# Output projection of an encoder trunk: eight blocks of full products, against two groups of seven products on chained weights

## The chip, the cores and the metric

One core of a Trainium2 chip runs the whole program. The metric is the device time of one execution in microseconds (us); the time before is the median of three runs, 1547.62 us (1545.86 to 1549.45).

## What is computed

A trunk of two layers works on 512 tokens of 1024 channels in float32. Each layer computes four branches (a convolution module and three kinds of attention), projects each to 1024 channels, mixes them by gates, applies one output projection and adds the residual; then a feed-forward block with a short convolution follows.

```python
h = _rmsnorm(x, g_mix[l])
proj = h @ w_in[l]
...
branch = jnp.einsum('bsnc,ncd->bsnd', ys, w_branch[l])
gates = jax.nn.sigmoid(gate_pre.reshape(bsz, seq, N_BRANCH, D_MODEL) + gate_b[l])
mixed = jnp.sum(gates * branch, axis=2)
x = x + mixed @ w_out[l]
x = x + _conv_ffn(_rmsnorm(x, g_ffn[l]), w_up[l], ffn_conv_w[l], ffn_conv_b[l], w_down[l])
```

The change concerns `mixed @ w_out[l]`: a product of 512 x 1024 with 1024 x 1024.

## The kernel before

**Layout.** Activations lie channel by channel: a tile has 128 channels on the partitions and the 512 tokens along it, so eight tiles hold one activation. A float32 product is made of three matmuls of rounded parts: high by high, high by low and low by high (`prod`, L274 to L279). So each weight and each activation is split into a high part, made by ScalarE (ACT), and a low part, made by VectorE (DVE).

**Weights.** They stream in units of 128 x 1024, two units ahead of use (`weights`, L226; `unit`, L262). SyncE's queue (SP) loads `w_raw` (two buffers), ACT makes `w_hi` (L256) and DVE makes `w_lo` (L258), with three buffers each. A buffer of w_hi or w_lo is free when the product that read it three units ago is done, and the instruction that fills it waits for that at its place in its engine's order.

**Gates.** For each of four branches and each of eight blocks d, PE makes the gate's pre-activation (24 matmuls into a `mm` bank), DVE scales it (`t`, L845), ACT takes the tanh (L847), PE makes the branch projection, DVE multiplies (L874), and GpSimd (POOL) adds the result to `mx` (L875; for the last branch's blocks 6 and 7, DVE does). With the last branch, block d of the mixture is complete, and ACT and DVE make its parts mh (L879) and ml (L880).

**Output projection** (in `layer`, L1466 to L1480). Eight blocks of output channels, each 8 x 3 matmuls of 512 columns, 192 a layer. The first two blocks are cut so that the last two mixed tiles are needed last. Behind each block `update` adds the residual (`xr`, loaded over SP's queue), writes the new residual (L929), and `norm_tile` prepares the next norm: ACT's xh (L339) and squares (L348), DVE's xl (L340) and sum of squares `sqacc` (L349). After the eighth, `broadcast_norm` sums the squares over the channels on PE (L367), and DVE runs Newton steps for the reciprocal root (L311 to L316) into `RB`.

**Up projection** (`ffn`). It begins with eight full blocks, whose results stay in `mm` banks until DVE has RB and evacuates them into `U` (L1081). Then come groups of seven products: for a 2 x 2 partition of weights and activations, seven products of combined parts replace eight. The seven weight combinations of a group are chained: A11 is loaded, split and used, then another quarter of the weights is added onto the same buffer by an accumulating load on POOL's queue (`grow`, L1123), which gives S3, then S2, then S4; likewise A22 gives S1 (`seven_unit`, L1126). One product is 24 matmuls of 256 columns and accumulates into one of three banks (A, B, C) of its group. ACT copies a bank to `sv` (L1007) before a later product accumulates further into it. The activations' combinations (`seven_forms`, L936) are made by DVE and ACT beside.

**Down sums.** The down projection needs sums of weight quarters, made in DRAM by 24 copying and accumulating transfers a layer on POOL's queue (`weight_sums`, L1148). They are dealt out during the attention and gates: each tick adds the pace (4.0, later 2.7) to a budget, and each transfer takes 11 from it.

**What sets the order.** A scheduler orders the instructions of each engine by priorities; weights stand high. Within an engine the order is then fixed, and an instruction that waits holds all behind it on that engine. PSUM has four `mm` and four `aux` banks.

## Time and profile before

| | |
|---|---|
| median of three runs | 1547.62 us (1545.86 to 1549.45) |
| the profiled execution | 1548.55 us, span 1546.8 us, mean PE clock 0.998 |
| busy share of the span | PE 99%, DVE 81%, ACT 58%, POOL 12% |
| output projection, layer 0 | 391.5 to 439.8 us |
| output projection, layer 1 | 1162.1 to 1205.6 us |
| first eight up blocks begin | 439.8 and 1205.6 us |

A row of a timeline gives the start in us, the duration, the engine, the line, the operation, what it writes and reads, and in brackets how long the engine was idle before and for whom it waited. PE is the matmul, PEld its weight load. The ends of matmuls are modelled, so a matmul's cost is read from the spacing of starts. A row of grouped instructions ends with total and mean time.

### The profile page before, as it was taken

How to read it: one execution, taken by the hardware profiler on the slowest of the kernel's cores; microseconds unless marked ns; L12 is line 12 of the kernel's file. 1: busy time of each engine (PE TensorE's matmuls, PEld its weight loads, DVE VectorE, ACT ScalarE, POOL GpSimd, SP SyncE). 2: the span in 40 equal slices, each digit the busy share in tenths (PEclk: the TensorE clock that was granted, in tenths of full speed). 3: DMA queues.
4: the chain of work that ended last, by engine and by line, in shares of the span. 5: the costliest groups of instructions: out<-in, count | busy, mean ns of one | idle time of the engine just before them, and what ended most of it. 6: DMA issues, size and time to landing. Idle time of an engine off the chain costs nothing.

```text
span 1546.8 us, 22163 instructions
## 1 busy us (share of the span) xinstructions
PE 1535.4 (99%) x7986; PEld 1313.9 (85%) x7986; DVE 1256.5 (81%) x2126; ACT 904.7 (58%) x1516; POOL 190.8 (12%) x276
## 2 busy tenths in 40 slices
PE   9999999999999999999999999999999999999998
PEld 8888888887789999888888888888888899988887
DVE  6689988764579998997586899887646899999974
ACT  6677777343456665564457777673334556655643
POOL 0113002222101110000001120022221011100000
PEclk9999999999999999999999999999999999999999
DMA  7767654647655886356558776546576589853675
GB/s 232 228 212 158 130 157 131 157 166 134 200 191 123 185 183 164 96 196 202 185 184 252 196 150 138 152 134 157 160 164 219 170 180 228 182 160 95 191 229 159
DMA packets 114142, 268.05 MB, mean 173 GB/s; under 512 B 26992, under 2 KB 28912, under 8 KB 114032
## 3 DMA queue, kind: packets, MB, share of 16 engines
q1 hardware_dynamic: 87664, 190.08, 38.4%
q0 software_dynamic: 26080, 76.03, 26.2%
q8 instruction: 63, 1.03, 0.3%
q10 hardware_dynamic: 288, 0.52, 0.1%
q14 instruction: 47, 0.39, 0.1%
HBM read 248.76 MB, written 58.72 MB: 199 GB/s over the span
## 4 chain that ended last, share of the span: by engine, by line
PE 88%; DMA 4%; DVE 4%; ACT 3%; issue 1%; POOL 0%; SPq 0%; ACTq 0%; DVEq 0%; POOLq 0%
PE mm L278 16%; PE mm L277 16%; PE mm L279 16%; PE aux L995 11%; PE aux L1240 3%; PE aux L1241 3%; PE aux L1242 3%; PE mm L506 2%; PE mm L507 2%; PE mm L508 2%; DMA chain<-W 2%; PE mm L1240 2%; PE mm L1241 2%; PE mm L1242 2%; PE aux L799 2%; DMA w_raw<-W 2%
## 5 line engine op out<-in xcount | busy, mean ns | idle before, releaser
L256 ACT ACTIVATE w_hi<-w_raw 128x1024 fp32r<-128x1024 f32 (+1 forms) x257 | 268.4, 1044 | 299.0 <-PE mm L278 142.0
L258 DVE TENSOR_TENSOR w_lo<-w_raw,w_hi 128x1024 fp32r<-128x1024 f32 (+1 forms) x257 | 310.1, 1208 | 87.2 <-ACT w_hi L256 85.3
L277 PE MATMUL mm<-xh,w_hi 128*128 128x512 f32 x896 | 350.5, 391 | 0.7 <-ACT w_hi L256 0.7
L279 PE MATMUL mm<-xh,w_lo 128*128 128x512 f32 x896 | 349.4, 390 | 0.5 <-DVE w_lo L258 0.5
L278 PE MATMUL mm<-xl,w_hi 128*128 128x512 f32 x896 | 349.4, 390 | 0.0
L279 PEld LDWEIGHTS mm<-xh,w_lo 128*128 128x128 f32 x896 | 168.2, 188 | 36.7 <-DVE w_lo L258 1.0
L277 PEld LDWEIGHTS mm<-xh,w_hi 128*128 128x128 f32 x896 | 168.3, 188 | 34.9 <-ACT w_hi L256 1.1
L278 PEld LDWEIGHTS mm<-xl,w_hi 128*128 128x128 f32 x896 | 168.4, 188 | 33.3
L995 PE MATMUL aux<-form,w_hi 128*128 128x256 f32 x768 | 140.2, 284 | 1.1 <-ACT sv L1007 1.1
L995 PEld LDWEIGHTS aux<-form,w_hi 128*128 128x128 f32 x768 | 120.0, 192 | 2.3 <-ACT sv L1007 1.9
L995 PE MATMUL aux<-form,w_lo 128*128 128x256 f32 x384 | 108.7, 283 | 0.0
L444 DVE SCALAR_TENSOR_TENSOR cv<-cv,prm 128x512 f32<-128x512 f32 x120 | 93.6, 780 | 0.7
L1036 ACT ACTIVATE cy<-U,prm 128x512 f32<-128x512 f32 x88 | 68.4, 808 | 31.8 <-DVE U L1081 21.0
L875 POOL TENSOR_TENSOR mx<-mx,t 128x512 f32<-128x512 f32 x44 | 65.2, 1489 | 167.7 <-DVE t L874 152.5
L845 DVE TENSOR_TENSOR t<-mm,RB 128x512 f32<-128x512 f32 x64 | 43.8, 685 | 45.0 <-PE mm L279 44.8
L506 PE MATMUL mm<-w_hi,xh 128*128 128x512 f32 x192 | 76.4, 398 | 0.4 <-DVE V L634 0.4
L507 PE MATMUL mm<-w_lo,xh 128*128 128x512 f32 x192 | 75.0, 391 | 0.0
L508 PE MATMUL mm<-w_hi,xl 128*128 128x512 f32 x192 | 74.8, 390 | 0.0
L1141 ACT ACTIVATE w_hi<-chain 128x1024 fp32r<-128x1024 f32 x48 | 50.7, 1057 | 39.9 <-DMA chain<-W 12.7
L995 PEld LDWEIGHTS aux<-form,w_lo 128*128 128x128 f32 x384 | 73.7, 192 | 0.0
L1150 POOL DMA_DIRECT2D sums<-W x36 | 31.8, 882 | 313.9 <-PE mm L279 165.6
L763 ACT ACTIVATE e<-e,rl 128x256 f32<-128x256 f32 (+2 forms) x96 | 57.4, 598 | 21.8 <-DVE rl L762 21.4
(343 smaller groups left out, 3469.0 us busy)
## 6 DMA issues: line engine op xcount, KB each, us to landing
w_raw<-W SPq DMA_DIRECT2D x199, 512.0 KB, 3.9
sums<-W POOLq DMA_DIRECT2D x24, 1024.0 KB, 11.0
chain<-W POOLq DMA_DIRECT2D x36, 512.0 KB, 5.6
w_raw<-W SPq DMA_DIRECT2D x66, 256.0 KB, 3.8
w_raw<-sums SPq DMA_DIRECT2D x44, 256.0 KB, 3.8
w_raw<-sums SPq DMA_DIRECT2D x22, 512.0 KB, 4.0
sums<-W POOLq DMA_DIRECT2D x12, 768.0 KB, 9.2
sums<-sums POOLq DMA_DIRECT2D x8, 1024.0 KB, 8.2
```

The source lines that it names most:

```text
L256: w = nc.scalar.activation(hi[:, s], raw[:, s], AF.Copy)
L258: nc.vector.tensor_tensor(lo[:, s], raw[:, s], hi[:, s].bitcast(F32), ALU.subtract)
L277: mm(ps, lhsT=wh, rhs=xh, start=start, stop=False)
L278: mm(ps, lhsT=wh, rhs=xl, start=False, stop=False)
L279: self.last_mm = mm(ps, lhsT=wl, rhs=xh, start=False, stop=stop)
L444: self.after_mm(v.scalar_tensor_tensor(acc, u[:, t:t + S], w(t), acc, ALU.mult, ALU.add))
L506: mm(pss[b], lhsT=self.Xh[k][:, t], rhs=hi[:, s], start=k == 0, stop=False)
L507: mm(pss[b], lhsT=self.Xh[k][:, t], rhs=lo[:, s], start=False, stop=False)
L508: self.last_mm = mm(pss[b], lhsT=self.Xl[k][:, t], rhs=hi[:, s], start=False, stop=k == KT - 1)
L995: self.last_mm = nc.tensor.matmul(o, lhsT=w[:, s], rhs=x, start=start and not (e or j or i), stop=j == 3 and i == 2, skip_group_check=True)
L1240: mm(ps, lhsT=x[0], rhs=w[0][:, cols], start=start, stop=False, skip_group_check=again)
L1241: mm(ps, lhsT=x[0], rhs=w[1][:, cols], start=False, stop=False, skip_group_check=again)
```

## The change

The output projection becomes two groups, `oa` and `ob` (output channels 0 to 511 and 512 to 1023), of seven products each, of the same kind as the up projection's: 14 products of 24 matmuls of 256 columns, 336 a layer. The order of the products is written out in `OUT_STEPS`; the first three are cut so that the last pair of mixed tiles is needed last. The weights are chained: A11's buffer has two of its own ("chain"), A22 and A12 use w_raw. The combinations of the mixed tiles are made in the gates of the last branch, by `mixed_forms` after each odd d. The residual is loaded by POOL's queue into four tiles before the last branch's end, and written by it. The norm tiles come in the order 0, 1, 4, 5, 2, 3, 6, 7, all behind the products S1 and S4. A down sums transfer takes 9 from the budget instead of 11.

```diff
+OUT_STEPS = [('oa', 'A11'), ('oa', 'A12'), ('ob', 'A11'), ('ob', 'A12'), ('oa', 'S3'), ('oa', 'A22'), ('ob', 'S3'),
+             ('ob', 'A22'), ('oa', 'S2'), ('oa', 'S1'), ('ob', 'S2'), ('ob', 'S1'), ('oa', 'S4'), ('ob', 'S4')]
...
-        self.Xh, self.Xl = [], []
+        self.Xh, self.Xl = [None] * KT, [None] * KT
...
+            if d % 2 == 1:
+                self.mixed_forms(d // 2)
+
+    def mixed_forms(self, j):
...
+        x, y = self.mixed[2 * j:2 * j + 2]
+        t = self.op.tile([P, 1024], F32, name="sums", tag="msum", bufs=1)
+        t1, t2, t3, t4 = (t[:, n * 256:(n + 1) * 256] for n in range(4))
+        b11, b12, b21, b22 = x[:, :256], x[:, 256:], y[:, :256], y[:, 256:]
+        v.tensor_tensor(t3, b12, b22, ALU.subtract)
+        v.tensor_tensor(t1, b11, b12, ALU.subtract)
+        v.tensor_tensor(t2, t3, b11, ALU.subtract)
+        v.tensor_tensor(t4, b21, t2, ALU.add)
+        hi, lo = (self.op.tile([P, 1024], F32R, name="mform", tag=f"mf{2 * j + n}", bufs=1) for n in range(2))
+        nc.scalar.activation(hi, t, AF.Copy, scale=0.5)
+        v.scalar_tensor_tensor(lo, t, 0.5, hi.bitcast(F32), ALU.mult, ALU.subtract)
...
+    def out_bank(self, g, n):
+
+        b = g, {'S3': 'B', 'A22': 'B', 'A12': 'C'}.get(n, 'A')
...
+    def out_part(self, g, n, w, js):
+
+        ps = self.out_bank(g, n)
+        for e in range(2):
+            o = ps[:, e * 256:(e + 1) * 256]
+            for j in js:
+                s = slice((2 * j + e) * P, (2 * j + e + 1) * P)
+                xh, xl = self.out_x(n, j)
+                for i, (a, x) in enumerate(((w[0], xh), (w[0], xl), (w[1], xh))):
...
+    def out_done(self, g, n):
...
+        if n in ('A11', 'S3', 'S2'):
+            tag, bufs = ("t1", 2) if n == 'S3' else ("th", 3)
+            t = self.svs[g, n] = self.gp.tile([P, S], F32, name="sv", tag=tag, bufs=bufs)
+            with self.first():
+                nc.scalar.activation(t, ps, AF.Copy)
+        if n == 'S2':
+            r, h = 1, 0
+            v.tensor_tensor(t, self.out_bank(g, 'S3'), t, ALU.subtract)
+        elif n == 'A12':
+            r, h, t = 0, 0, self.svs[g, 'A11']
+            v.tensor_tensor(t, t, ps, ALU.add)
+        elif n == 'S1':
+            r, h, t = 1, 1, self.svs[g, 'S3']
+            with self.first():
+                v.tensor_tensor(t, t, ps, ALU.subtract)
+        elif n == 'S4':
+            r, h, t = 0, 1, ps
...
+        v.tensor_tensor(o, two(t), o, ALU.add)
+        if h:
+            for e in range(2):
+                xn = x[:, e * S:(e + 1) * S]
+                nc.gpsimd.dma_start(self.xnew[d + e], xn)
+                self.norm_tile(d + e, xn, self.op)
+
+    def out_projection(self):
...
+                self.nc.gpsimd.dma_start(x[:, e * S:(e + 1) * S], self.xres[d + e])
...
             if n == 'A11':
-                raw = self.fp.tile([P, 1024], F32, name="chain", tag="w_more", bufs=2)
+                pool, tag = (self.op, "chain") if g in ('oa', 'ob') else (self.fp, "w_more")
+                raw = pool.tile([P, 1024], F32, name="chain", tag=tag, bufs=2)
...
-                yield 11
+                yield 9
...
-                for d in range(0, KT, 2):
...
-                            if k1 == KT:
-                                self.update(d + e, pss[e], self.op)
+                self.out_projection()
```

Three places of the order follow, where numbers behind a name tell tiles apart. The first is ACT in the output projection. Before, each weight split stands alone, among the parts of the norm (xh, sq):

```order
L256 ACTIVATE w_hi<-w_raw 128x1024
L339 ACTIVATE xh_4264<-xn,prm 128x512
L348 ACTIVATE sq<-xn 128x512
L256 ACTIVATE w_hi<-w_raw 128x1024
L339 ACTIVATE xh_4306<-xn,prm 128x512
L348 ACTIVATE sq<-xn 128x512
```

After, in the same place, from the split of S2 of group oa (w_hi_4421) to that of S4 of group ob (w_hi_4605); sv_4419 is the copy of ob's S3, sv_4478 that of oa's S2, and w_hi_4450, 4482, 4527 and 4559 are S1 of oa, S2 and S1 of ob, and S4 of oa:

```order
L1249 ACTIVATE w_hi_4421<-chain_4076 128x1024
L1249 ACTIVATE w_hi_4450<-w_raw_4324 128x1024
L944 ACTIVATE sv_4419<-aux_4394 128x512
L1249 ACTIVATE w_hi_4482<-chain_4217 128x1024
L1249 ACTIVATE w_hi_4527<-w_raw_4387 128x1024
L944 ACTIVATE sv_4478<-aux_4198 128x512
L1249 ACTIVATE w_hi_4559<-chain_4076 128x1024
L1249 ACTIVATE w_hi_4605<-chain_4217 128x1024
```

A copy now stands behind one or two weight splits, each of which waits for a buffer that PE still reads. PE's order there is A22 of oa, 9 matmuls of S3 of ob, 5 of S2 of oa, A22 of ob, 19 of S2 of oa, 13 of S2 of ob, S1 of oa, 11 of S2 of ob, 4 of S4 of oa, S1 of ob, 20 of S4 of oa, S4 of ob; ahead of these, 10 of S3 of oa, 2 of S3 of ob, 14 of oa, 13 of ob.

The second place is DVE around the first evacuation of the up projection (U) and the last Newton step (rs_q, RB). Before:

```order
L315 TENSOR_TENSOR rs_q<-rs_q,ms 128x512
L258 TENSOR_TENSOR w_lo<-w_raw,w_hi 128x1024
L316 SCALAR_TENSOR_TENSOR RB<-rs_q,RB 128x512
L961 TENSOR_TENSOR forms<-xf,forms 128x256
L1081 TENSOR_TENSOR U_4490<-mm,RB 128x512
L1081 TENSOR_TENSOR U_4493<-mm,RB 128x512
L964 TENSOR_TENSOR form<-forms,form 128x1024
```

After:

```order
L321 TENSOR_TENSOR rs_q<-rs_q,ms 128x512
L1250 TENSOR_TENSOR w_lo<-chain,w_hi 128x1024
L322 SCALAR_TENSOR_TENSOR RB<-rs_q,RB 128x512
L1067 TENSOR_TENSOR forms<-forms,xf 128x256
L1188 TENSOR_TENSOR U_4702<-mm,RB 128x512
L1068 TENSOR_TENSOR forms<-xf,forms 128x256
L1188 TENSOR_TENSOR U_4705<-mm,RB 128x512
```

The w_lo in front of the last Newton step is now that of the first chained product (chain, L1250), which follows the fourth up block on PE and takes a buffer that this block reads; before, it stood five rows behind the first U (L1142), and the one in front belonged to a full block. On PE, 16 matmuls of that chained product now stand between the fourth and the fifth block.

The third place is POOL in the last branch's gates, with the last transfers of the down sums. Before:

```order
L875 TENSOR_TENSOR mx<-mx,t_3895 128x512
L1150 DMA sums_681<-W 512x512
L875 TENSOR_TENSOR mx<-mx,t_3945 128x512
L875 TENSOR_TENSOR mx<-mx,t_3994 128x512
L1150 DMA sums_682<-W 384x512
L875 TENSOR_TENSOR mx<-mx,t_4050 128x512
L875 TENSOR_TENSOR mx<-mx,t_4099 128x512
```

After:

```order
L880 TENSOR_TENSOR mx<-mx,t_3447 128x512
L1258 DMA sums_681<-W 512x512
L880 TENSOR_TENSOR mx<-mx,t_3529 128x512
L1258 DMA sums_682<-W 384x512
L880 TENSOR_TENSOR mx<-mx,t_3580 128x512
L880 TENSOR_TENSOR mx<-mx,t_3658 128x512
L880 TENSOR_TENSOR mx<-mx,t_3703 128x512
```

The last transfer is followed by two adds before and by nine after; the residual's eight loads (L976) stand a few rows further ahead, between adds.

More of the change, by code (lines that the diff above doesn't have):

```diff
@@ L110, in weight_units @@
                 units.append(('branch', (n, d // 4), 1024))
-    for d in range(8):
-        units.append(('out', d, 1024))
+    units.extend(('quarter', (key, r, c), 1024) for key in ('oa', 'ob') for r in range(2) for c in range(2))
     for g in range(NP2):
@@ L143, in pack_weights @@
                 g, r, c = a
-                src = w_up[l].reshape(4, 2, P, 2, NP2, 2, P)[:, c, :, 1 - r, g].transpose(1, 0, 2, 3)
+                if g in ('oa', 'ob'):
+                    src = w_out[l].reshape(4, 2, P, 2, 2, 2, P)[:, c, :, 'ab'.index(g[1]), 1 - r]
+                else:
+                    src = w_up[l].reshape(4, 2, P, 2, NP2, 2, P)[:, c, :, 1 - r, g]
+                src = src.transpose(1, 0, 2, 3)
             elif kind == 'quad':
@@ L147, in pack_weights @@
             else:
-                w, c = {'in_d': (w_in, a), 'up': (w_up, a), 'out': (w_out, 0 if kind != 'out' else a * P)}[kind]
+                w, c = {'in_d': (w_in, a), 'up': (w_up, a)}[kind]
                 src = w[l][:, c:c + P].reshape(8, P, P).transpose(1, 0, 2)
@@ new lines, in out_x @@
+    def out_x(self, n, j):
+        form = {'S1': 0, 'S2': 1, 'S3': 2, 'A22': 3}.get(n)
+        if form is not None:
+            return [t[:, form * 256:(form + 1) * 256] for t in self.mforms[j]]
+        r, h = {'A11': (0, 0), 'A12': (1, 0), 'S4': (1, 1)}[n]
+        return [t[:, h * 256:(h + 1) * 256] for t in self.MH[2 * j + r]]
+    def out_bank(self, g, n):
+        b = g, {'S3': 'B', 'A22': 'B', 'A12': 'C'}.get(n, 'A')
+        if b not in self.banks:
+            self.banks[b] = self.mm() if b[1] == 'C' else self.aux()
+        return self.banks[b]
@@ new lines, in out_part @@
+    def out_part(self, g, n, w, js):
[6 more added lines that the diff above has]
+                for i, (a, x) in enumerate(((w[0], xh), (w[0], xl), (w[1], xh))):
+                    start = n in ('S3', 'A11', 'A12') and not (e or j or i)
+                    self.last_mm = self.nc.tensor.matmul(o, lhsT=a[:, s], rhs=x, start=start, stop=j == 3 and i == 2,
+                                                         skip_group_check=True)
@@ new lines, in out_done @@
+    def out_done(self, g, n):
+        nc = self.nc
+        v = nc.vector
+        ps = self.out_bank(g, n)
+        if n in ('A11', 'S3', 'S2'):
[15 more added lines that the diff above has]
+            r, h, t = 0, 1, ps
+        else:
+            return
+        d = 4 * 'ab'.index(g[1]) + 2 * (1 - r)
+        x = self.residual[d // 2]
+        two = lambda t: t.rearrange("p (e q) -> p e q", e=2)
+        o = two(x)[:, :, h * 256:(h + 1) * 256]
+        v.tensor_tensor(o, two(t), o, ALU.add)
[4 more added lines that the diff above has]
+                self.norm_tile(d + e, xn, self.op)
@@ new lines, in out_projection @@
+    def out_projection(self):
+        self.banks, self.svs, self.residual = {}, {}, []
+        for d in range(0, KT, 2):
+            x = self.op.tile([P, 1024], F32, name="xr", tag=f"xr{d}", bufs=1)
+            for e in range(2):
+                self.nc.gpsimd.dma_start(x[:, e * S:(e + 1) * S], self.xres[d + e])
+            self.residual.append(x)
+        ws = []
+        for js in ((0, 1, 2), (3,)):
+            for i, (g, n) in enumerate(OUT_STEPS[:3]):
+                if js[0] == 0:
+                    ws.append(self.unit())
+                self.out_part(g, n, ws[i], js)
+                if js[0] == 3:
+                    self.out_done(g, n)
+        for g, n in OUT_STEPS[3:]:
+            self.out_part(g, n, self.unit(), range(4))
+            self.out_done(g, n)
@@ L1167, in weight_sums @@
                 add(part(t, d), part(src, s), accum_op=ALU.add)
-                yield 11
+                yield 9
         for d, b, s in ((s2, s3, b21), (s4, s2, b22)):
@@ L1365, in run @@
                         self.w_list.append((n, lambda src=src: [src]))
+                self.w_list.extend(('seven', (l, g, n)) for g, n in OUT_STEPS)
                 for kind, a, b in UP_STEPS:
@@ L1426, in layer @@
         last = l == L - 1
-        self.Y, self.mixed, self.MH, self.glu_u = [None] * 4, [], [], []
+        self.Y, self.mixed, self.MH, self.mforms, self.glu_u = [None] * 4, [], [], [], []
         with tc.tile_pool(name="gate", bufs=1, reuse_waits="tile") as self.gp:
@@ L1465, in layer @@
                 self.start_norm('g_ffn')
-                for d in range(0, KT, 2):
-                    cuts = (0, KT - 2, KT) if d == 0 else (0, KT)
-                    pss, ws = [self.mm(), self.mm()], []
-                    for k0, k1 in zip(cuts, cuts[1:]):
-                        for e in range(2):
-                            if k0 == 0:
-                                ws.append(self.unit())
-                            hi, lo = ws[e]
-                            for k in range(k0, k1):
-                                s = slice(k * P, (k + 1) * P)
-                                self.prod(pss[e], hi[:, s], lo[:, s], self.MH[k][0], self.MH[k][1], k == 0,
-                                          k == KT - 1)
-                            if k1 == KT:
-                                self.update(d + e, pss[e], self.op)
+                self.out_projection()
                 self.xres = self.xnew
```

10 lines of the change are left out of this document (6 added, 4 removed).

## The prediction

> **What bounds the kernel now.** I read the chain of work that ended last first: it says which engine sets the end.
>
> ```profile
> PE 88%; DMA 4%; DVE 4%; ACT 3%; issue 1%; POOL 0%; SPq 0%; ACTq 0%; DVEq 0%; POOLq 0%
> ```
>
> TensorE (PE) sets the end, so a microsecond counts only if PE has fewer columns to stream or waits less. Second, what PE waits for over the whole span (total, times, longest):
>
> ```profile
> PE mm L277 <- ACT mh L879: 2.5, 1, 2.5
> ...
> PE aux L995 <- ACT sv L1007: 1.1, 2, 0.8
> PE mm L277 <- ACT w_hi L256: 0.7, 1, 0.7
> PE mm L279 <- DVE w_lo L258: 0.5, 1, 0.5
> ```
>
> PE hardly waits anywhere; of what it does wait, the mh, w_hi and w_lo rows (3.7 us) belong to one place, at the output projection. Third, four stretches with each engine's busy time (instructions), the PE clock, the DMA share and GB/s: the output projection of layer 0, the 22 us behind it, the same two of layer 1, and a piece of the first.
>
> ```profile
> 391.50:439.80 48.30, 45.72 (x194) 37.12 (x193) 29.63 (x37) 19.78 (x27) 5.42 (x12) 0.96 0.63 206
> 439.80:462.10 22.30, 22.30 (x100) 18.44 (x100) 20.18 (x33) 14.00 (x19) 0.54 (x1) 1.00 0.52 177
> 1162.10:1205.60 43.50, 43.50 (x193) 36.04 (x192) 26.74 (x34) 18.14 (x26) 4.46 (x12) 1.00 0.67 220
> 1205.60:1228.00 22.40, 22.40 (x100) 18.55 (x99) 20.29 (x34) 14.11 (x19) 0.54 (x1) 1.00 0.58 199
> 392.00:404.00 12.00, 9.42 (x34) 7.05 (x33) 8.06 (x10) 4.40 (x6) 1.54 (x5) 0.86 0.28 98
> ```
>
> Layer 1's projection has no hole: 43.5 us, PE busy throughout. Layer 0's is 4.8 us longer. Behind it DVE is busy 90% of the time (20.2 of 22.3), in it about 60%.
>
> **PE's stream.** The projection is now 192 matmuls of 512 columns a layer and becomes 2 x 7 x 24 = 336 of 256. The spacing of each kind, from the first and last of 18 and of 16 matmuls in a row:
>
> ```profile
> 435.76 0.39 PE L277 MATMUL mm<-mh,w_hi 128*128 128x512 f32 x1
> ...
> 439.61 0.39 PE L279 MATMUL mm<-mh,w_lo 128*128 128x512 f32 x1
> ```
> ```profile
> 539.77 0.28 PE L995 MATMUL mm<-xh,w_lo 128*128 128x256 f32 x1
> ...
> 541.57 0.28 PE L995 MATMUL mm<-xh,w_lo 128*128 128x256 f32 x1
> ```
>
> 3.85/17 = 0.2265 us and 1.80/15 = 0.120 us. So 192 x 0.2265 = 43.5 becomes 336 x 0.120 = 40.3: 3.2 us less a layer, not the eighth (5.4) that the column count says, since the narrow matmul costs more per column. [...]
>
> **New waits inside the stage.** I walk the after order with these durations: what passes from PE to ACT to DVE when a weight buffer comes free, and from PE to ACT when a bank is copied.
>
> ```profile
> 439.39 0.39 PE L278 MATMUL mm<-ml,w_hi 128*128 128x512 f32 x1
> 439.61 0.39 PE L279 MATMUL mm<-mh,w_lo 128*128 128x512 f32 x1
> 439.81 1.06 ACT L256 ACTIVATE w_hi<-w_raw 128x1024 fp32r<-128x1024 f32 x1 [3.24 <-PE mm L278]
> 440.91 1.22 DVE L258 TENSOR_TENSOR w_lo<-w_raw,w_hi 128x1024 fp32r<-128x1024 f32 x1 [0.18 <-ACT w_hi L256]
> 442.05 0.74 DVE L340 SCALAR_TENSOR_TENSOR xl<-xn,prm,xh 128x512 fp32r<-128x512 f32 x1
> ...
> 547.33 0.28 PE L995 MATMUL aux<-form,w_lo 128*128 128x256 f32 x1
> 547.66 0.59 ACT L1007 ACTIVATE sv<-aux 128x512 f32<-128x512 f32 x1
> ```
>
> ACT starts 0.42 after the releasing 512-wide matmul and 0.33 after a 256-wide one, so 0.21 after its slot ends. w_hi's last reader is a product's last matmul but one: ACT splits w_hi from 0.09 after the product's end, done at 1.15 (PE may go at 1.20); DVE's w_lo is done at 2.4 (PE at 2.45). A copy (0.59) behind a w_hi on ACT comes at 0.09 + 0.97 + 0.59 + 0.05 = 1.7. DVE starts its next operation 1.14 after a 1024-wide one. What PE has in between, by the after order:
>
> - S2a's weights wait for A22a's buffer. Cover: 9 matmuls of S3b = 1.08. Wait 0.12 for w_hi; two matmuls later (1.44) 1.0 for w_lo: **1.1**.
> - S4a's weights wait for S1a's. Cover: 11 of S2b and two of S4a = 1.56; but two 512-wide DVE operations of S1a's result stand ahead of the w_lo, which comes at 0.21 + 2 x 0.60 + 1.22 + 0.05 = 2.7: 1.1. Then S1b needs the copy of S2b, which ACT makes behind two w_hi, at 1.32 + 1.7 = 3.0, and PE is there at 2.9: 0.1 to 0.2. **1.3**.
> - S3a to A22a, and S2a to S1a: the copy at 1.7, cover 13 matmuls = 1.56: **0.13** each.
> - The head. The forms of the mixed rows stand on DVE in front of the second group's weights.
>
> ```profile
> 458.92 0.68 DVE L316 SCALAR_TENSOR_TENSOR RB<-rs_q,RB 128x512 f32<-128x512 f32 x1
> 459.52 0.41 DVE L961 TENSOR_TENSOR forms<-xf,forms 128x256 f32<-128x256 f32 x1
> 459.86 1.28 DVE L1081 TENSOR_TENSOR U<-mm,RB 128x512 f32<-128x512 f32 x2
> ```
> ```profile
> 1161.11 1.30 POOL L875 TENSOR_TENSOR mx<-mx,t 128x512 f32<-128x512 f32 x1 [5.31 <-DVE t L874]
> ```
>
> A 512-wide operation takes 0.60, a 256-wide 0.34. In layer 1 the first form that needs mx5 can go when POOL has it, at 1162.41. From there to the end of A12b's w_lo DVE has 7 operations of 256, 6 of 512 and 3 of 1024: 2.4 + 3.6 + 3.4 = 9.4, at 1171.9. PE, started at 1162.1, wants it after 74 matmuls (8.9), at 1171.0. With 0.2 to 0.4 for ACT's parts in between: **1.3**.
>
> Sum 1.1 + 1.3 + 0.3 + 1.3 = **4.0** a layer. From below 1.3 (the head alone, if ACT and DVE run ahead), from above 6: DVE goes from 26.7 to about 40 busy of 44 us (six more w_lo, 6 x 1.14, and some three forms, each 4 x 0.34 + 1.14), so any slip stays. I take the walked value.
>
> **Behind the stage.** In the old kernel the fifth up block takes a bank that U's first evacuation frees, at 459.86 + 0.64 = 460.5, ahead of need (PE waits for nothing in that stretch). In the new order the w_lo of the first chained up product stands ahead of the last Newton step and of U on DVE, and waits until the fourth block has released its buffer. From that block's end: w_hi released at 0.42 less two slots, so at -0.03, done at 1.03; w_lo 1.07 to 2.29; last Newton step, form and U (2.21 + 0.60 + 0.34 + 0.68): 3.8. PE holds 16 matmuls of the chained product for it (1.9), which themselves wait for the same w_hi (1.08) and w_lo (1.0). They end at 4.0: **2.1** lost. Add **0.2** for the last norm tiles, now four at the end instead of one, whose xl the first up block needs. From below 0.2, from above 3.5.
>
> Both layers alike: -3.2 + 4.0 + 2.3 = +3.1, twice = **+6.2**.
>
> **Layer 0's stall.** Three rows show where it comes from, and the clock behind it; then the DMA issues (count, size, median us to landing) in the 45 us ahead of the projection, of layer 0 and of layer 1.
>
> ```profile
> 380.12 1.06 ACT L256 ACTIVATE w_hi<-w_raw 128x1024 fp32r<-128x1024 f32 x1 [6.22 <-DMA w_raw<-W]
> ...
> 392.71 1.06 ACT L256 ACTIVATE w_hi<-w_raw 128x1024 fp32r<-128x1024 f32 x1 [5.24 <-DMA w_raw<-W]
> ...
> 397.75 0.63 PE L277 MATMUL mm<-mh,w_hi 128*128 128x512 f32 x1 [2.49 <-ACT mh L879]
> ...
> 401.51 0.39 PE L279 MATMUL mm<-mh,w_lo 128*128 128x512 f32 x1
> ```
> ```profile
> w_raw<-W SPq DMA_DIRECT2D x6, 512.0 KB, 9.5
> sums<-W POOLq DMA_DIRECT2D x2, 1024.0 KB, 15.0
> ```
> ```profile
> w_raw<-W SPq DMA_DIRECT2D x8, 512.0 KB, 4.1
> sums<-W POOLq DMA_DIRECT2D x1, 1024.0 KB, 11.6
> ```
>
> The weights land late beside the down sums' transfers, ACT waits, and mh comes late. From 397.75 to 401.51 eight matmuls take 3.76 instead of 1.81: after a wait of 2.5 the clock was halved for that long, 1.95 us. The place costs 4.8 (48.3 - 43.5) + 0.7 + 0.5 = **6.0**. With 9 instead of 11 a step the sums end seven POOL adds earlier in the order, and two of these adds stand 6.8 apart:
>
> ```profile
> 1140.71 1.28 POOL L875 TENSOR_TENSOR mx<-mx,t 128x512 f32<-128x512 f32 x1 [1.46 <-DVE t L874]
> 1147.51 1.29 POOL L875 TENSOR_TENSOR mx<-mx,t 128x512 f32<-128x512 f32 x1 [5.51 <-DVE t L874]
> ```
>
> That is about 48 us: the last sums transfer is gone before the late stretch begins. Against it: layer 1 has sums there too and no stall. The residual's loads, 2 MB, now come over POOL's queue in the stretch that the sums leave. I take the 6.0 whole, with the other end, 0, as a rival.
>
> **Costed at nothing.** The chained weights are accumulating loads, of which the up stage has 36; the last column is their median time to landing.
>
> ```profile
> chain<-W POOLq DMA_DIRECT2D x36, 512.0 KB, 5.6
> ```
>
> The eight new ones a layer take 5.6 us each and then 1.06 + 1.22 for the split, against four products (11.5) between two uses of one chain. The residual's loads and writes leave SP's queue for POOL's, whose adds are off PE's path until mx5; 14 weight transfers of 512 KB replace 8, and 2 MB of loads leave the stage: about 1 MB more in 44 us, 24 GB/s on 220. If these covers go, a late chain costs up to 2 us a layer.
>
> **Sum:** 1548.55 (the profiled execution; span 1546.8 and the rest around it) + 6.2 - 6.0 = **1548.8**. The median of the runs is 0.9 below that execution, with 3.6 between the runs; I leave the sum there.
>
> **Rivals.** (1) *Faster: the waits don't show.* In the up stage the same chained products run with the same copies, and PE lost 1.1 us in two waits over two layers. If the fill covers here too, only the head stays: -3.2 + 1.3 + 0.2 = -1.7 a layer, with layer 0's 6.0: 1539.2. Against it: the covers counted above (1.1, 1.6, 1.9) are shorter than 2.45, and the chained w_lo stands ahead of U. Chance 0.25. (2) *Slower: the clock falls at the new stalls.* Place: behind the fourth up block, 1.1 + 1.0 of waiting in 4 us; price 1.95 a layer as at 397.75; it decides if two short waits count like one of 2.5. 1548.8 + 3.9 = 1552.7. [...] Chance 0.17. (3) *No relief:* the late weights of layer 0 aren't the sums' doing or move elsewhere: 1548.55 + 6.2 = 1554.8. For it: layer 1. Against: landing 9.5 against 4.1 with two to three sums transfers in the stretch. Chance 0.18.
>
> **How the numbers follow.** Forecast 0.40, its own range 1545.5 to 1552 (waits 1.5 us a layer either way). The range for 8 in 10, 1540 to 1556, leaves out the lower half of (1) and the tail of (3). 0.2%, about what a measurement can tell, is 3.1 us: below 1544.5 or above 1550.7. Faster: 0.25 + 0.02 = 0.27. Slower: 0.10 of the forecast, 0.14 of (2), 0.17 of (3) = 0.41. Same: 0.32.
>
> **What would show it.** Right: a projection of 44 to 45 us in both layers, PE waits on w_lo at S2a, S4a and A12b of about 1 us each, and a wait on w_hi, then w_lo, behind the fourth up block; layer 0 as long as layer 1. Wrong: projection near 41 (rival 1), clock under 1 behind the stage (2), layer 0's stretch ahead still with w_raw at 9 us (3), or waits on the chain's DMA, which I priced at nothing.

## The result, and the profile after

The changed kernel takes 1565.63 us (median of four runs, 1563.95 to 1571.04) against 1547.67 us (1545.86 to 1549.45): a ratio of 1.0116, 95% interval 1.0104 to 1.0128, so 18 us slower. The forecast was 1548.8 in a range of 1540 to 1556. The profiled execution is the slowest of the four, 1571.04, with a span of 1569.3. A second profile of the same kernel, below called "again", has a span of 1561.0.

What PE waits for in the changed kernel (total, times, longest) answers to the same view of before:

```profile
PE aux L1102 <- DVE w_lo L1250: 6.3, 3, 3.0
PE aux L932 <- DVE w_lo L1250: 3.7, 4, 1.1
PE aux L932 <- ACT sv L944: 3.6, 2, 1.9
PE aux L1102 <- ACT w_hi L1249: 3.5, 2, 2.3
PE mm L932 <- DVE w_lo L1250: 1.6, 2, 0.8
PE mm L932 <- DVE ml L885: 1.4, 2, 0.7
```

L932 is the output projection. L1102 is the chained up products; all but 0.3 us of its rows stands at the first of them, behind the fourth up block. The old waits of layer 0 (mh, w_hi and w_lo of the full blocks, 3.7 us) are gone; 20 us of new ones stand there, half in the projection and half behind it. The stretches, with each engine's busy time, the clock, the DMA share and GB/s; of each layer first the projection, then from its end to the fifth up block; first the profiled execution, then again, then the kernel before with only the pace of the down sums changed:

```profile
389.50:439.50 50.00, 44.99 (x338) 43.43 (x337) 35.40 (x46) 25.35 (x33) 9.41 (x12) 0.93 0.62 137
439.50:470.40 30.90, 26.59 (x116) 21.36 (x115) 27.61 (x45) 18.61 (x26) 7.56 (x17) 0.92 0.72 244
1169.60:1218.80 49.20, 43.98 (x338) 42.38 (x338) 35.36 (x46) 25.20 (x32) 9.39 (x12) 0.97 0.62 139
1218.80:1250.90 32.10, 26.61 (x116) 21.39 (x115) 27.64 (x46) 18.77 (x27) 7.44 (x17) 0.94 0.74 251
```
```profile
389.90:435.40 45.50, 42.18 (x337) 40.79 (x337) 35.13 (x46) 25.14 (x32) 9.43 (x12) 1.00 0.66 150
435.40:467.00 31.60, 26.77 (x117) 21.52 (x116) 27.82 (x46) 19.05 (x28) 7.54 (x17) 0.93 0.73 240
1166.30:1211.80 45.50, 42.18 (x337) 40.80 (x336) 35.11 (x46) 25.16 (x32) 9.36 (x12) 1.00 0.68 150
1211.80:1243.50 31.70, 26.62 (x116) 21.42 (x115) 27.68 (x46) 18.80 (x27) 7.41 (x17) 0.90 0.76 255
```
```profile
389.50:433.00 43.50, 43.50 (x194) 36.02 (x193) 26.70 (x34) 18.16 (x26) 4.41 (x12) 1.00 0.70 223
433.00:455.20 22.20, 22.20 (x100) 18.38 (x99) 20.15 (x33) 13.91 (x19) 0.54 (x1) 1.00 0.51 175
```

Read the third against the second. The projection is 45.5 us instead of 43.5. From its end to the fifth up block PE needs 31.6 instead of 22.2, and the 16 chained matmuls done there account for 1.9 of it: 7.5 us lost. Together 9.5 a layer, 19 in two; the down sums give back 4.8 (first experiment, by its ratio); that leaves 14, where again was measured at 15.1 (1564.63 against 1549.51). Span against span, again is 20.7 us longer than the third profile (1561.0 against 1540.3): 19, and 1.4 more in the fifth up block, whose first matmuls still run at half clock (0.43 us apart instead of 0.23). The first execution has 4.5 and 3.7 us more in its two projections. So three things are to be explained: 2 us in the projection, some 4 more in some executions, and 7.5 behind it.

**Behind the projection.** Two things come late. The first is the norm. All eight norm tiles now stand behind S1 and S4, and the sum of squares that the norm starts from is complete later; ACT's copy of it (sqh), before and after:

```profile
443.43 0.63 ACT L362 ACTIVATE sqh<-sqacc 128x512 fp32r<-128x512 f32 x1 [1.42 <-DVE sqacc L349]
```
```profile
449.23 0.63 ACT L367 ACTIVATE sqh<-sqacc 128x512 fp32r<-128x512 f32 x1 [1.29 <-DVE sqacc L354]
```

That is 3.6 us behind the projection's end before and 9.8 after; both kernels show the same in layer 1. The first U, the end of the norm's chain, started 20.1 us behind the projection and now starts 28.6 to 29.8 behind it. So 6.2 of some 9 us are there when the norm begins, and the rest, 2.5 to 3.6, comes on its way.

The second is the reload. POOL before:

```profile
416.65 0.57 POOL L946 DMA_DIRECT2D xf<-res  x1 [6.95 <-DMA res<-xn]
...
443.28 0.54 POOL L946 DMA_DIRECT2D xf<-res  x1 [4.86 <-DMA res<-xn]
```

And the timeline of the changed kernel in layer 0, POOL, ACT, DVE and PE:

```profile
443.55 2.14 POOL L967 DMA_DIRECT2D res<-xr  x4 [4.42 <-DVE xr L963]
...
451.33 0.54 POOL L1053 DMA_DIRECT2D xf<-res  x1 [4.44 <-DMA res<-xr]
452.05 2.78 POOL L1053 DMA_DIRECT2D xf<-res  x5 [0.19 <-issue]
```
```profile
457.59 2.09 ACT L1060 ACTIVATE xf<-xf,prm 128x512 f32<-128x512 f32 x3 [1.21 <-DMA xf<-res]
459.58 1.05 ACT L262 ACTIVATE w_hi<-w_raw 128x1024 fp32r<-128x1024 f32 x1
...
462.70 1.04 ACT L1249 ACTIVATE w_hi<-chain 128x1024 fp32r<-128x1024 f32 x1
```
```profile
460.66 1.23 DVE L264 TENSOR_TENSOR w_lo<-w_raw,w_hi 128x1024 fp32r<-128x1024 f32 x1 [0.94 <-ACT w_hi L262]
...
466.01 1.22 DVE L1250 TENSOR_TENSOR w_lo<-chain,w_hi 128x1024 fp32r<-128x1024 f32 x1
...
468.09 0.68 DVE L1188 TENSOR_TENSOR U<-mm,RB 128x512 f32<-128x512 f32 x1
```
```profile
463.80 0.38 PE L1102 MATMUL aux<-xh,w_hi 128*128 128x256 f32 x1 [1.16 <-ACT w_hi L1249]
...
467.29 0.58 PE L1102 MATMUL aux<-xh,w_lo 128*128 128x256 f32 x1 [2.98 <-DVE w_lo L1250]
...
468.09 0.41 PE L1102 MATMUL aux<-xh,w_lo 128*128 128x256 f32 x1
468.30 0.41 PE L1102 MATMUL aux<-xh,w_hi 128*128 128x256 f32 x1
```

The up projection's forms read the residual back from DRAM (`seven_forms`, `xf`). Before, it was written block by block, and one reload followed each write, the first at 409 us. Now six of its eight loads are issued at 451 to 455 us, behind the last writes. ACT's scalings of xf then stand, waiting, ahead of two weight splits; DVE waits for the first of these, does the forms and Newton steps queued behind it, and starts the chained w_lo 3.3 us after its w_hi was begun. PE waits 1.2 and 3.0 us, and when it goes on, one 256-wide matmul takes 0.21 us instead of 0.12. Two slices of 5 us show the clock behind it:

```profile
465.00:470.00 5.00, 2.71 (x12) 2.72 (x13) 4.97 (x10) 1.19 (x2) 0.90 (x1) 0.52 0.22 24
470.00:475.00 5.00, 5.00 (x20) 4.20 (x20) 5.00 (x9) 3.19 (x4) 0.00 (x0) 0.80 0.43 81
```

Of the first slice PE works 2.7 us at half speed (1.3 lost); the second loses 1.0.

The spacing of PE's starts in again says what the 7.5 us are: 5.0 in layer 0 and 5.2 in layer 1 are the two waits (for the chained w_hi and w_lo), 0.7 goes in the first up block, whose matmuls meet the last norm tiles, and some 1.7 are the matmuls at half clock or just behind a wait.

**In the projection, in some executions.** ACT and POOL of the changed kernel, then PE, and then ACT of again:

```profile
423.78 1.06 ACT L1249 ACTIVATE w_hi<-chain 128x1024 fp32r<-128x1024 f32 x1 [3.10 <-PE aux L932]
427.10 1.06 ACT L1249 ACTIVATE w_hi<-chain 128x1024 fp32r<-128x1024 f32 x1 [2.26 <-DMA chain<-W]
428.06 0.58 ACT L944 ACTIVATE sv<-aux 128x512 f32<-128x512 f32 x1
```
```profile
419.47 0.89 POOL L1231 DMA_DIRECT2D chain<-W  x1 [4.90 <-DVE w_lo L1250]
```
```profile
426.50 0.39 PE L932 MATMUL aux<-mh,w_lo 128*128 128x256 f32 x1 [1.08 <-DVE w_lo L1250]
426.72 0.28 PE L932 MATMUL aux<-mh,w_hi 128*128 128x256 f32 x1
428.69 0.80 PE L932 MATMUL aux<-mform,w_hi 128*128 128x256 f32 x2 [1.69 <-ACT sv L944]
429.29 0.41 PE L932 MATMUL aux<-mform,w_lo 128*128 128x256 f32 x1
```
```profile
424.21 1.06 ACT L1249 ACTIVATE w_hi<-chain 128x1024 fp32r<-128x1024 f32 x1 [3.10 <-PE aux L932]
425.53 1.06 ACT L1249 ACTIVATE w_hi<-chain 128x1024 fp32r<-128x1024 f32 x1 [0.26 <-PE aux L932]
426.50 0.58 ACT L944 ACTIVATE sv<-aux 128x512 f32<-128x512 f32 x1
```

The load that makes ob's S4 out of its S2 is issued at 419.47, when S2's w_lo is done, and has landed at 427.1, 7.6 us later; ACT's split waits for it, and the copy `sv`, which PE needs for S1 of ob, stands behind that split. Two waits of 1.1 and 1.7 us with one pair of matmuls between them halve the clock once more (granted 0.50 from 428.7 to 433.0). In again the load is in time, ACT waits only for PE's buffer, and the wait on the copy is absent in both layers. The profiles of all versions that keep this load, 14 with two layers each, show it late in 9 of 28 projections: ACT's split then begins 6.7 to 7.8 us behind the issue, else at most 5.7.

### The profile page after: what moved, and what is told of

The parts are those of the page before. It is cut to its first block, busy times and chain, and to the rows that moved or that the text cites. A ratio compares the mean times of both kernels' runs of the same rounds, so it can differ in the third digit from the quotient of the medians.

```text
span 1569.3 us, 22886 instructions
## 1 busy us (share of the span) xinstructions
PE 1542.2 (98%) x8274; PEld 1330.1 (85%) x8274; DVE 1297.0 (83%) x2190; ACT 931.4 (59%) x1548; POOL 225.5 (14%) x324
## 3 DMA queue, kind: packets, MB, share of 16 engines
q0 software_dynamic: 30944, 92.81, 29.8%
## 5 line engine op out<-in xcount | busy, mean ns | idle before, releaser
L262 ACT ACTIVATE w_hi<-w_raw 128x1024 fp32r<-128x1024 f32 (+1 forms) x241 | 251.3, 1043 | 241.9 <-PE mm L284 84.6
L264 DVE TENSOR_TENSOR w_lo<-w_raw,w_hi 128x1024 fp32r<-128x1024 f32 (+1 forms) x241 | 291.3, 1210 | 76.8 <-ACT w_hi L262 75.3
L1102 PE MATMUL aux<-form,w_hi 128*128 128x256 f32 x768 | 140.0, 283 | 0.0
L1102 PEld LDWEIGHTS aux<-form,w_hi 128*128 128x128 f32 x768 | 120.0, 192 | 0.7 <-ACT sv L1114 0.4
L1102 PE MATMUL aux<-form,w_lo 128*128 128x256 f32 x384 | 108.7, 283 | 0.0
L1250 DVE TENSOR_TENSOR w_lo<-chain,w_hi 128x1024 fp32r<-128x1024 f32 x64 | 78.0, 1220 | 28.4 <-ACT w_hi L1249 28.2
L1249 ACT ACTIVATE w_hi<-chain 128x1024 fp32r<-128x1024 f32 x64 | 67.4, 1055 | 56.5 <-DMA chain<-W 21.8
L1231 POOL DMA_DIRECT2D chain<-W x48 | 42.3, 881 | 258.3 <-DVE w_lo L1250 251.0
L1102 PEld LDWEIGHTS aux<-form,w_lo 128*128 128x128 f32 x384 | 73.7, 192 | 0.0
```

What stands on the lines that cost most here:

```text
L262: w = nc.scalar.activation(hi[:, s], raw[:, s], AF.Copy)
L264: nc.vector.tensor_tensor(lo[:, s], raw[:, s], hi[:, s].bitcast(F32), ALU.subtract)
L1102: self.last_mm = nc.tensor.matmul(o, lhsT=w[:, s], rhs=x, start=start and not (e or j or i), stop=j == 3 and i == 2, skip_group_check=True)
L1250: nc.vector.tensor_tensor(lo, raw, hi.bitcast(F32), ALU.subtract)
```

## The experiments

Times of a group of runs are compared with the kernel before on the same chip, 1548.9 to 1549.7 us there. The changed kernel was measured again in one of these groups, with a ratio of 1.0107 (1.0082 to 1.0133).

**The down sums' pace alone.** In the kernel before:

```diff
-                yield 11
+                yield 9
```

> The kernel before with 9 instead of 11 a transfer of the down sums, and nothing else: one part of the change alone. Theory A (the sums' transfers make layer 0's weights late): the stall ahead of and in layer 0's output projection goes, 6 us, about 1541.7. Rival (that lateness is not the sums' doing or only moves): within 1.5 us of 1547.7.

1543.03 us, ratio 0.9969 (0.9955 to 0.9983), which is 4.8 us; the medians differ by 5.8 (1548.86 in its group). PE's waits of layer 0 are gone and its projection is 43.5 us like layer 1's. In the 45 us ahead of it there is no sums transfer left, and the weights land in 3.4 us, where they took 9.5:

```profile
w_raw<-W SPq DMA_DIRECT2D x8, 512.0 KB, 3.4
```

Theory A holds. This is also the fastest version of all, faster than both kernels.

**The reload without its wait on the writes.** The forms read the residual of before the projection:

```diff
-                nc.gpsimd.dma_start(x[:, e * S:(e + 1) * S], self.xres[2 * j + e])
+                nc.gpsimd.dma_start(x[:, e * S:(e + 1) * S], self.xold[2 * j + e])
```

> The changed kernel in the same order of instructions, but the up projection's forms read the residual of before the output projection (so those forms hold other numbers), and their eight loads wait for no write. Theory A (behind the stage the late reload of the residual holds ACT, and with it the weight splits, Newton and U): PE's waits there, 4.1 and 5.3 us, fall to about 2.1 each and the halved clock behind them goes in part, 1555 to 1560. Rival B (the chained w_lo ahead of U on DVE is the whole cause): the waits stay, within 1.5 us of the changed kernel.

1562.51 us, ratio 1.0088 (1.0065 to 1.0110): not told apart from the changed kernel, and PE's waits behind the stage stay (1.7 and 3.0 the longest). But it was a weak test: the loads still stand behind the writes' issue on POOL, and ACT scaled the first xf at 450 us, 14.4 us after the projection's end. It told nothing against the reload.

**S4 without the accumulating load.**

```diff
-        if n[0] == 'A':
+        own = g in ('oa', 'ob') and n == 'S4'
+        if n[0] == 'A' or own:
...
+            nc.sync.dma_start(raw, q(1, 2) if own else q(int(n[1]), int(n[2])))
...
-        if more:
+        if more and not (g in ('oa', 'ob') and n == 'S2'):
```

> The changed kernel, but S4 of both output groups uses a quarter loaded over SP's queue instead of the accumulated chain, and the accumulating load on S2 is left out (the output projection's numbers are others). Theory A (the accumulating load of ob's S4 lands late, ACT's split of it waits, and the copy of S2 that PE needs stands behind that): PE's wait on the copy, 1.7 and 1.9 us, falls under 0.5 and the halved clock after it, some 2.4 us each, goes: 1557 to 1562. Rival (the order on ACT alone makes that wait): the wait stays, within 1.5 us of the changed kernel.

1566.56 us, ratio 1.0116 (1.0101 to 1.0131): no gain. The wait on the copy is gone in this profile and the projection 45.5 us in both layers, but behind it the fifth block starts 33 to 34 us after the projection's end instead of 31.6, of which 1.0 is eight more chained matmuls ahead of it: the four more loads over SP's queue take w_raw's two buffers, and the up blocks' weights come late (PE waits 1.0 and 1.5 us for the w_hi of a full block, and not at all in again). And since again shows 45.5 us with the accumulating load too, the absence can't be put down to this edit. What it shows is the price of the other way to load.

**U ahead of the chained w_lo.** The split of the first chained up product is put behind the first U (`u0`):

```diff
-        nc.scalar.activation(hi, raw, AF.Copy)
-        nc.vector.tensor_tensor(lo, raw, hi.bitcast(F32), ALU.subtract)
+        with self.tc.issue_after(self.u0.ins) if (g, n) == (SEVEN[0], 'A11') else nullcontext():
+            nc.scalar.activation(hi, raw, AF.Copy)
+            nc.vector.tensor_tensor(lo, raw, hi.bitcast(F32), ALU.subtract)
```

> The changed kernel, but the first chained up product's weights are split only behind the first evacuation of U, which takes the w_lo out of the way of the last Newton step; PE then has no chained product to fill the wait. Theory B (this order is the cause of the stall behind the stage): the stall falls to 1 us or so, 1553 to 1558. Theory A (the reload holds ACT and DVE anyway): U comes only 1.1 us earlier and the fill of 1.9 us is lost, within 3 us of the changed kernel.

1567.29 us, ratio 1.0118. PE now waits 7.5 us (3.7 the longest) for U itself; the fifth block starts at 29.1 and 29.4 us, 2.4 and 2.3 earlier than in again, of which 1.7 are 14 chained matmuls that are not done by then. Theory B, that the order of w_lo and U is the cause, is out: U itself starts only 0.8 to 0.9 us earlier.

**The changed kernel again.**

> The changed kernel once more, for a second profile. Theory A (the accumulating load of ob's S4 lands at the edge of its need): the wait on the copy of S2 differs between executions, so it can be absent here, and the output projection is then 45.5 instead of 49 to 50 us; the stall behind the stage stays at 30 to 32 us from the projection's end to the fifth block. Rival: both as in the first profile.

1564.63 us, ratio 1.0107. As shown above: no wait on the copy, projection 45.5 us twice, fifth block at 31.5 and 31.7 us. Theory A on the accumulating load holds so far that its lateness comes and goes; what makes it land in 7.6 us in one execution and in at most 5.6 in another was not found; the transfers issued in the next 8.5 us are the same in both profiles, one weight load and two residual writes.

**Forms from xh.** No reload and no scaling:

```diff
-                for e in range(2):
-                    s = slice(e * S, (e + 1) * S)
-                    nc.scalar.activation(x[:, s], x[:, s], AF.Copy, scale=self.par('g_ffn', 2 * j + e))
...
+                x, y = (t.bitcast(F32) for t in self.Xh[2 * j:2 * j + 2])
```

> The changed kernel, with the up projection's forms made from the high part xh, which lies in SBUF, so the reload of the residual (eight loads) and ACT's eight scalings are left out, and the low part is missing in those forms. Theory A (the late reload holds ACT and DVE): U comes about 2.5 us earlier after the projection's end (29.5 to 27), PE's wait there falls from 4.5 to 5.6 to about 2 us, and if that is under what halves the clock, 3 us more go: 4 to 6 us a layer, 1554 to 1558. Rival C (DVE's sum of work and the late norm set U): the fifth block starts within 1 us of where it did, 1563 to 1566.

1559.60 us, ratio 1.0065 (1.0048 to 1.0081): 5 us less. The fifth block starts at 29.1 and 29.9 us, PE waits there about 3 us a layer instead of 5 (3.7 + 2.4 in its rows for both), but the clock still falls (256-wide matmuls behind the waits 0.21 us apart instead of 0.12 in both layers). DVE is now busy with hardly a gap (0.2 us in layer 0) from the norm's first step to U: a second part of the lateness is its own work.

**The forms' subtractions on POOL.**

```diff
-                v.tensor_tensor(t3, b12, b22, ALU.subtract)
+                nc.gpsimd.tensor_tensor(t3, b12, b22, ALU.subtract)
```

(and the other three of a form)

> The changed kernel with the four subtractions and additions of each of the up projection's forms on POOL instead of DVE, the reload as it was. Theory C (DVE's work between the norm and U sets the stall): DVE has 2.7 us less to do ahead of U, the fifth block starts about 2 to 3 us earlier, 1558 to 1562. Theory A (the reload): U still waits for nothing that the reload holds on DVE once the forms are off it, so it gains too, by the idle time of 1.8 to 3.2 us on DVE; the two differ in whether DVE's idle time ahead of U (A) or its busy time (C) shrinks.

1577.46 us, ratio 1.0185: both theories missed. A 256-wide operation takes POOL 0.7 to 1.7 us where DVE needs 0.34, ACT's form split waits for it, and the chained w_hi stands behind that on ACT:

```profile
468.04 1.06 ACT L1070 ACTIVATE form<-forms 128x1024 fp32r<-128x1024 f32 x1 [3.58 <-POOL forms L1068]
469.00 1.04 ACT L1249 ACTIVATE w_hi<-chain 128x1024 fp32r<-128x1024 f32 x1
```

It tells nothing on A against C, but shows again that whatever waits ahead of a split on ACT is what PE waits for.

**Both edits, xh and S4's plain load.**

> Both edits at once: forms from xh and S4's plain load (numbers of both differ). If the two causes are separate, the projection is 45.5 us in both layers and the stall behind as in the run with xh alone: 1553 to 1557. If removing one only moves the wait to the other, as the S4 run alone did, it stays above 1562.

1565.77 us, ratio 1.0107: the gain of xh is lost. The fifth block is at 31.5 and 34.0 us, behind 24 chained matmuls as in the S4 run, and in layer 0 the split of S4 waited 1.8 us for its plain load over SP. So that place is short of time whichever way the weight comes.

**U without the norm.** U is multiplied by a tile that is ready:

```diff
-                v.tensor_tensor(self.U[b][:, a % 2, 1:513], ps, self.RB, ALU.mult)
+                v.tensor_tensor(self.U[b][:, a % 2, 1:513], ps, self.Xh[0].bitcast(F32), ALU.mult)
```

> The changed kernel, but U is multiplied by a tile that is there (xh of block 0) instead of RB, so the up blocks wait for no norm; the norm is still made (U holds other numbers). Theory D (what is lost behind the stage is the late norm: the last four norm tiles end 6 us later than before, and all that follows comes late): the stall there goes, 7 us a layer with the clock that falls behind it, 1549 to 1553, and the projection stays at 45.5. Rival (weight buffers or loads set the stall, whatever U waits for): waits on w_hi or w_lo of 2 us and more stay behind the fourth block, above 1558.

1565.46 us, ratio 1.0102. The fifth block starts at 23.3 and 23.2 us, so the norm was what it waited for; but then PE waits 3 us for the second U, which stands on DVE behind the chained w_lo, and that behind the norm's steps and the forms, which are all still there. The stall moved by a block and the time didn't change; this profile also has the late S4 load in layer 1 (projection 49.0) and a wait of 2.2 us for a copy in the up stage.

**One and two chained products early.**

```diff
-    return steps[:-2] + own[:1] + steps[-2:] + own[1:] + [('free',) + w[1:] for w in after[:2]] + after[2:]
+    return steps[:4] + own[:1] + steps[4:] + own[1:] + [('free',) + w[1:] for w in after[:2]] + after[2:]
```

(for two, the first product of the next group goes to the second place of `own`, and both stand behind the fourth block)

> The changed kernel with the first chained up product placed behind the fourth block in the list of steps instead of the sixth, so its weights are split before two blocks that can't run yet. Theory D: U comes at about 29 to 30 us after the projection as in the run with U ahead, but PE has 24 instead of 16 matmuls for it and no wait for their weights in between: the fifth block starts 2 to 2.5 us earlier and 8 matmuls (1 us) more are done, 1557 to 1560. Rival: no change, above 1562.

> As the run before, with the first product of the next group placed there too: 24 matmuls more (2.9 us) to fill the wait for U. Theory D: another 2 to 2.9 us a layer, and the wait left (1 to 2 us) may no longer halve the clock: 1548 to 1555. If DVE is what falls behind through these splits ahead of U, the gain is lost: 1557 to 1560.

With one, 1566.92 us (ratio 1.0112): 24 matmuls are done where 16 were, without waiting for their weights, but the rest is one wait of 3.6 and 3.9 us for U, and the clock falls as before (512-wide matmuls behind it 0.43 us apart instead of 0.23). The fifth block starts at 29.6 and 29.9 us, so with the eight matmuls more the place is some 2.8 us a layer better than in again, yet the time is no better. In this profile the late S4 load takes it back in layer 0 (projection 50.3), and in layer 1 a copy in the up stage that PE waits 2.1 us for; why all four executions lie within 1.3 us is not shown. With two, 1560.82 us (1.0075, 1.0047 to 1.0102): what is left of the wait is 0.7 and 1.7 us, and the mean clock of the whole span is 1.000. That profile is the fastest of four executions (1557.23 to 1564.87); the slower three have a clock of 0.997 to 0.999.

**Two early, and xh.**

> Two chained products early and the up projection's forms from xh (no reload; their low part is left out). Theory D: the reload gave 2 us of U's lateness and the fill covers the rest, so hardly any stall is left: 1546 to 1551, about the kernel before, since what is left is the projection at 45.5 instead of 43.5 twice, less the 5 us of the sums. Rival: not under 1554.

1551.61 us (ten executions), ratio 1.0018 (1.0008 to 1.0028), 0.6 above the forecast's end. The fifth block starts at 29.3 and 29.2 us with 48 chained matmuls (5.8) done, PE waits 0.3 us for U in each layer, and the mean clock is 1.000:

```profile
465.19 0.47 PE L284 MATMUL mm<-xh,w_hi 128*128 128x512 f32 x1 [0.27 <-DVE U L1182]
```

So with the stall covered and the reload gone, the changed projection costs about what the sums give back. It is 13.0 us under again, so the stall behind the projection is most of the 18 us.

**U without the norm, with all full blocks first.** The same multiplication as above, and `steps + own` as the list.

> The changed kernel with U multiplied by xh of block 0 instead of RB (its numbers are others), and with all eight full blocks ahead of the first chained product. Theory D (the stall is the late norm's, through U): the fifth block starts 22.2 to 23 us after the projection's end and PE loses nothing behind the stage, 1549 to 1553. Rival (weight splits stall PE there by themselves): 2 us and more of waits on w_hi, w_lo or a bank stay in that stretch.

1566.65 us, ratio 1.0106. The fifth block is at 23.3 and 23.1 us, and again PE waits 2.3 and 3.6 us for the second U, which stands behind the w_lo of a later full block. Theory D missed. The rival's sign came, a wait of 2 us and more for a bank, but it is U that frees the bank: the test moved the block on DVE instead of taking it away.

**The forms behind U.** Their work is begun behind the first U:

```diff
-        self.side.append(work())
+        self.forms_work = work()
...
+                if self.forms_work:
+                    self.side.append(self.behind(u, self.forms_work))
+                    self.forms_work = None
```

(`behind` runs each piece of it under `issue_after` of U)

> The changed kernel with the up projection's forms (reload, scaling, subtractions) put behind the first evacuation of U; the same work and the same numbers. Theory E (the late norm becomes a stall because the forms and their reload stand between the Newton steps): U comes at 23 to 24 us after the projection, the fifth block at about 23.5, so 6 us a layer less than in the changed kernel after its fill is taken off, 1551 to 1555, unless the forms then come late for the first S3 product. Rival C' (norm and weight splits alone are as late): above 1560.

1564.02 us, ratio 1.0096 (1.0081 to 1.0111). The fifth block is at 26.8 and 28.8 us instead of 23.5, with none and two of the chained matmuls done. The scalings of the reload are still ahead of the weight splits on ACT, and DVE waits for the split between two Newton steps; ACT first, then DVE:

```profile
455.30 1.34 ACT L1060 ACTIVATE xf<-xf,prm 128x512 f32<-128x512 f32 x2 [0.76 <-DMA xf<-res]
456.55 1.04 ACT L262 ACTIVATE w_hi<-w_raw 128x1024 fp32r<-128x1024 f32 x1
```
```profile
457.62 1.23 DVE L264 TENSOR_TENSOR w_lo<-w_raw,w_hi 128x1024 fp32r<-128x1024 f32 x1 [2.53 <-ACT w_hi L262]
```

This is the reload's price on its own in layer 0, 2.5 us of DVE's time, with the forms out of the way. The same place shows that a wait need not halve the clock. PE waits 3.6 us for U, and the matmuls behind it run at full speed (spacing 0.22 to 0.31 us; at half clock it is 0.43):

```profile
462.50 0.47 PE L283 MATMUL mm<-xh,w_hi 128*128 128x512 f32 x1 [3.60 <-DVE U L1195]
462.81 0.40 PE L284 MATMUL mm<-xl,w_hi 128*128 128x512 f32 x1
```

In layer 1 two waits of 1.5 and 3.6 us did halve it (0.43 us apart behind them).

> The run before with two chained products early. Theory E: no stall is left to fill, so it is the same as the run before or up to 2 us less, 1550 to 1554; what is left over the kernel before with its 5 us of the sums taken off is the projection, 2 us a layer, and what the forms cost later.

With two chained products early, 1559.56 us (1.0062): no wait above 0.2 us is left between the projection and the fifth block, which comes at 28.9 and 28.7 us with 48 chained matmuls (5.8) done. But the forms are now late for the first S3, where PE waits up to 1.3 us, and copies in the up stage cost 2.6: what is moved past U is owed later.

**The forms from xh and behind U.** Both edits.

> Both edits at once: the up projection's forms from xh (no reload, no scaling; their low part is left out) and behind the first evacuation of U. Theory F (the late norm alone costs little; the reload on ACT and the forms on DVE, which it now meets, make the stall): U at about 23 to 24 us behind the projection, the fifth block within 1 us of 22.2 plus what little chained work stands there, waits behind the stage under 1.5 us a layer and no halved clock, 1548 to 1553. Rival D (the late norm by itself makes the stall): U at 26 us or later, above 1556.

1557.63 us, ratio 1.0048 (1.0031 to 1.0065). In layer 0 DVE does the norm with nothing but weight splits between, U comes 22.9 us behind the projection and the fifth block at 23.7 (25.9 in layer 1), and PE waits 0.4 and 1.3 us for U:

```profile
PE mm L283 <- DVE U L1188: 1.7, 2, 1.3
```

The clock stays at 1.00 there. Theory F holds for layer 0: with the norm as late as in the changed kernel (sqh at 9.9 us) but only weight splits in its way, the place costs 1.5 us, and the reload on ACT and the forms on DVE, which the late norm meets, make the rest of the 7.5. In layer 1 it is 3.7: there two transposes of the residual for the kernel's output have come between the Newton steps on DVE, and the first waits 1.4 us for its load. This division holds for this order alone. In the kernel before, the same forms and reload stood among the Newton steps and PE waited for nothing there; the norm began 6.2 us earlier. The time is above the 1548 to 1553 expected: this profile has the late S4 load in layer 0 again (projection 48.6), and copies in the up stage wait 2.6.

## Why the prediction was wrong, by its steps

1. **PE's stream, -3.2 a layer: right.** Of the 45.5 us of the projection in again, 4.2 are waits, and 1.0 is nine single matmuls that start 0.1 to 0.2 late, four of them just behind a wait; 40.3 are left for 336 matmuls.
2. **Waits inside the stage, 4.0: right in places and in sum (4.2).** Measured 0.95 and 0.94 at the head (1.3 foretold), 1.0 at S2a (1.1), 1.25 at S4a (1.1 and 0.2). The foretold projection of 44.3 is 45.5; the missing us is that of the late matmuls of step 1.
3. **"Costed at nothing", the accumulating loads: wrong in 9 of 28 projections.** 5.6 us from the row of the up stage was used with four products between two uses. But S4's load can only start when S2's w_lo is done, late in that time, and landed after 7.6; I had named up to 2 us a layer for a late chain, and in the first profile it cost 4.5 and 3.7. A late load also holds the copy behind its split on ACT, which I had placed behind two splits and not behind a load.
4. **"Behind the stage", 2.1 + 0.2: the step that failed.** I counted from the fourth block's end, took the chained w_lo to run "1.07 to 2.29" behind it, as soon as its buffer is free, and one Newton step, a form and U to follow by 3.8. So I took the rest of the norm to be done by then, and the last norm tiles stood in the sum with 0.2. In the profile w_lo started 3.5 us after the block's end (462.5, and 466.0 in the row above), and U was done at 6.3. The norm began 6.2 us later behind the projection than before. The late residual's loads and writes were "costed at nothing" as a change of queue; that the up stage reads the residual back, and that ACT and DVE queue on it, was not in the walk at all. Against 2.3 stand 7.5 us, of which 5 are waits, 0.7 the last norm tiles and 1.7 slow matmuls.
5. **Layer 0's stall, -6.0: right.** The sums' pace alone gives -4.8 by the ratio (0.9969) and -5.8 by the medians.
6. **The clock (rival 2): it came, and on top.** It was priced at 1.95 a layer where PE waits 2.1; PE waited twice that. Its chance of 0.17 was my estimate. With waits of 1.1 and 1.7 us, a pair of matmuls between (changed kernel, layer 0), the granted clock fell to 0.50, and so it did behind the single wait of 2.5 in the kernel before (0.50 from 399.75 to 401.2), but not in every run (last section). With waits of 0.7 and 0.8 us at the head of again (0.95 and 0.94 by the starts), 2.6 us apart, it stayed at 1.00.

Rivals 1 and 3 are out: the waits show, and the relief came.

Left open: why the accumulating load takes at most 5.6 us in one execution and 7.6 in the next, and what decides whether a wait halves the clock. A projection that writes its last norm tiles earlier wasn't tried; it would show directly how much of the stall the late norm makes.

## What to carry to other kernels

A step that finishes its results in another order changes what everybody who reads them meets: follow each result to all its readers, the ones that go through memory too, and ask what is queued behind the reader on its engine. Results that are all finished at the end of a step start the next chain late, even if the step itself is shorter. A gain of 3 us in the bound engine's stream is small beside what one late split costs there, since in these runs a single wait of 2.3 to 3.9 us brought a halved clock with it in seven of eight places. And when a change has several parts, the one that pays can be the smallest: here it was a number in the pace of a background transfer.

## What the runs showed of the hardware

- The clock fell after short waits that stand close together. In ten projections a wait of 1.1 us, two matmuls and a wait of 0.9 to 1.9 us followed on each other; in eight the matmuls behind ran at half clock (256-wide ones at 0.21 instead of 0.12 us; granted 0.50 in the changed kernel, layer 0), and 1.4 to 2.8 us were lost. It did not fall with 0.9 us (forms behind U, two early, layer 1: granted 1.00 over the projection), and once not with 1.4 (two early, and xh, layer 1: still 0.12 us apart), though 1.2 was enough in two others.
- A single wait of 2.3 to 3.9 us halved it in seven of eight places (512-wide matmuls behind it 0.43 us apart instead of 0.23), with 1.5 to 2.9 us lost; one of 3.6 us did not (forms behind U, layer 0: 0.22 to 0.31 apart), nor did one of 1.7 (two chained early, layer 1: 0.22 to 0.30).
- A 256-wide subtraction took POOL 0.7 to 1.7 us (the forms' subtractions on POOL), DVE 0.34 from start to start.
- An accumulating load of 512 KB landed in 7.6 us or in at most 5.6 in the same place of the same program, in two executions (ob's S4 of layer 0, the changed kernel and again).
